# Expert stages of a two-layer trunk on one core: slot indices two units ahead, the transposed activations copied by ScalarE, folded stream factors, and one more weight buffer

## The chip, the core and the metric

The kernel runs on one core of a Trainium2 chip. The core has five instruction streams that run side by side and meet at semaphores: TensorE (PE in the profile, with its weight loads as PEld), VectorE (DVE), ScalarE (ACT), GpSimd (POOL) and SyncE (SP, which here issues nearly all DMAs). Matmul results land in PSUM, everything else lies in SBUF, and the weights are in HBM. The metric is the device time of one execution in microseconds (us); lower is better.

## The reference, cut to what matters

```python
def hier_moe(h, wg_r, bg_r, we_r, be_r, w_gate, w_up, w_down):
    # h: (T, 1024). Top-1 of 4 expert groups, then top-2 of the 8 experts in it.
    ...
    def expert(args):
        xb, e = args
        return (jax.nn.silu(xb @ w_gate[e]) * (xb @ w_up[e])) @ w_down[e]
    ys = lax.map(expert, (xs, blk_e)).reshape(slots, d)
    ys = ys * slot_w[:, None]
    return jax.ops.segment_sum(ys, slot_tok, num_segments=t + 1)[:t]

for layer in range(2):
    ...                                   # a mixer: even layer, odd layer
    x = x + mx[2] * yx
    if need_ctx:                          # layer 0: 256 latent and 256 context tokens
        y = hier_moe(tokens, *moe_params)
        x = x + mx[5] * y[:256]; xc = xc + mc[5] * y[256:]
    else:                                 # layer 1: 256 latent tokens
        x = x + mx[5] * hier_moe(hx2, *moe_params)
```

All is float32. Each layer has 32 experts, with three matrices of 2 MB each (gate and up 1024x512, down 512x1024), so a layer reads 201 MB of expert weights.

## The kernel before, in words

The program runs the even mixer, the expert stage of layer 0, the odd mixer, and the expert stage of layer 1, in this order; the text calls the two expert stages "layer 0" and "layer 1". The change touches the expert stages alone.

**Slots and units.** Each expert has 64 slots for the tokens sent to it. A **unit** is two experts, 128 slots; 16 units make a layer. In layer 0 a further unit of one expert (the fourth in order, the "extra" one) takes an expert that overflows its 64 slots. For a unit the kernel needs an **index**: `group` (L453) compares positions with slot numbers and gives, for four experts, one 0/1 tile `gt` per 128 tokens; `slot_sums` (L263) multiplies them with token numbers and routing weights on PE into the PSUM bank `mx`, DVE copies the sums out (L264) and makes the row list `ix` (L272) and the slot weights `ws` (L309), and POOL gathers the rows from HBM into one of two buffers `xg` (L275). `turned` transposes the rows on PE (L288) into `xT`.

**A unit on PE.** `hidden(j)` multiplies expert j's gate and up weights (L329, L330; 8 contraction steps c); ACT takes the silu (`sg`, L333), DVE the product `a` (L334). `turn` transposes `a` on PE into `mx` (L348), and a copy (L350) brings it to SBUF as `aT`. `down` multiplies with the down weights (L364) into the two banks `y`. Then ACT and DVE split `y` times the slot weight into two parts `yh`, `yl` (L378, L379), and `scatter` sends them back to the tokens: for each 128 tokens two pairs of matmuls with the 0/1 matrix `S` (L387, L388; `S` itself is made by `places`, L484 and L342), and the sum into `x_sb`. In layer 0 the result is first multiplied with a factor that depends on the stream, latent or context (`mx5`: L392), then added (L393, half of it on POOL). In layer 1 there is one stream, and the factor is folded into `y` (L373).

**The order on PE** is written out by hand (`manual_schedule`); the other engines' order is set by the build's scheduler, and each engine then takes its instructions strictly in that order. In step k of the main loop PE runs `hidden(0)` of unit k, with hooks after contraction step c (the index of unit k+1 at c=1, a scatter at c=3 and c=7), then `turn` and `down` of unit k-1, then `hidden(1)` of unit k with the transposes of the gathered rows of unit k+1. So a unit's down part stands in the middle of the next unit.

**Weights** come as 1 MB loads (L145) on SP's queue, six per expert, into a ring of buffers: 5 `w` and 8 `wx` in layer 0 (`NW`, `NX[0]`), 5 and 11 in layer 1. A load waits until PE is done with the buffer it overwrites. The order of the loads is that of use: gate and up of a unit's first expert, the four down loads of the unit before, gate and up of the second expert.

Of the kernel before, what the change touches and what calls it, by code (L numbers as in the profile page):

```python
# [34 lines left out]
NE = 32  # L35
# [2 lines left out]
GRP = 4  # L38
NW = 5
NX = (8, 11)  # L40
NZ = (0, 0)
EXTRA = 3
RP = 300
HP = 300
# [16 lines left out]
class Trunk:  # L61
# [247 lines left out]
            nc.vector.tensor_add(ws[r], wl[r, a:a + 1], wl[r, b:b + 1])  # L309
        return ws  # L310

    def unit(self, W, xT, slots, ws, posbc, NT, x_sb, mx5, last=False):

        nc = self.nc
        T = NT * 128
        u = {}

        def hidden(j, hooks=()):  # L320
            if "a" not in u:
# [22 lines left out]
        def turn():  # L344
            M = len(W()) * CAP
            pt = self.mps.tile([128, 512], F32, name="mx", bufs=1)
            for c in range(4):
                nc.tensor.transpose(pt[:, c * M:(c + 1) * M], u["a"][:M, c:512:4], self.ident[:M, :M])  # L348
            aT = u["aT"] = self.mp.tile([128, 4, M], F32, name="aT", bufs=2)
            nc.vector.tensor_copy(aT, pt[:, :4 * M].rearrange("p (c m) -> p c m", c=4))  # L350

        def down():
            ne = len(W())
            M = ne * CAP
            mz = mx5
            if last and len(mx5) == 2:
                mz = self.slot_mx5(u["S"], mx5)
            y = [self.mps.tile([128, 512], F32, name="y", bufs=2) for h in range(2)]
            for cc in range(2):
                for h in range(2):  # L360
                    for c in (2 * cc, 2 * cc + 1):
                        for j in range(ne):
                            r = slice(64 * j, 64 * j + 64)
                            nc.tensor.matmul(y[h][r], u["aT"][:, c, r], W()[j][2][cc][:, c % 2, 512 * h:512 * h + 512],  # L364
                                             start=(c == 0), stop=(c == 3))
            w = ws()[:M]
            ys = []
            for h in range(2):
                yh = self.mp.tile([128, 512], F32R, name=f"yh{h}", bufs=1)
                yl = self.mp.tile([128, 512], F32R, name=f"yl{h}", bufs=1)  # L370
                if len(mz) == 1:
                    yv = self.mp.tile([128, 512], F32, name="tm", bufs=2)
                    nc.vector.scalar_tensor_tensor(yv[:M], y[h][:M], w, mz[0][:M, 512 * h:512 * h + 512], op0=OP.mult,  # L373
                                                   op1=OP.mult)
                    nc.scalar.activation(yh[:M], yv[:M], AF.Copy)  # L375
                    (nc.vector if last else nc.gpsimd).tensor_tensor(yl[:M], yv[:M], f32(yh[:M]), op=OP.subtract)  # L376
                else:
                    nc.scalar.activation(yh[:M], y[h][:M], AF.Copy, scale=w)  # L378
                    nc.vector.scalar_tensor_tensor(yl[:M], y[h][:M], w, f32(yh[:M]), op0=OP.mult, op1=OP.subtract)  # L379
                ys.append((yh, yl))  # L380

            def scatter(t):
                for h, (yh, yl) in enumerate(ys):
                    i = 2 * t + h
                    s = u["S"][:M, t * 128:(t + 1) * 128]
                    p = self.mps.tile([128, 512], F32, name="gu" if last and i % 4 > 1 else "sc", bufs=2)
                    nc.tensor.matmul(p, s, yh[:M], start=True, stop=False)  # L387
                    nc.tensor.matmul(p, s, yl[:M], start=False, stop=True)  # L388
                    xv = x_sb[:, t, 512 * h:512 * h + 512]
                    if len(mz) == 2:  # L390
                        tm = self.mp.tile([128, 512], F32, name="tm", bufs=2)
# [12 lines left out]

    def slot_mx5(self, S, mx5):

        nc = self.nc
        v = self.mp.tile([128, 2], F32, name="sv")
        nc.vector.tensor_reduce(v, f32(S).rearrange("p (s t) -> p s t", s=2), axis=AX.X, op=OP.add)
        m = self.mp.tile([128, 8, 128], F32, name="xT", bufs=2).rearrange("p c n -> p (c n)")  # L410
# [29 lines left out]
    def moe(self, l, NT, pos, whl, counts, weights, first, posT, x_sb, mx5, early):  # L440
# [7 lines left out]
        def group(g):  # L448

            gts[g] = []  # L450
            for t in range(NT):
                x = self.mp.tile([128, GRP, CAP], F32R, name="gt", bufs=2 * NT)
                nc.vector.tensor_tensor(x, self.slotrow, pos[:, t, g * GRP:(g + 1) * GRP, None]  # L453
                                        .to_broadcast([128, GRP, CAP]), op=OP.is_equal)
                gts[g].append(x.rearrange("p a b -> p (a b)"))

        def inputs(p, ahead=True, banks=("xg",)):

            gt = [x[:, 128 * (p % 2):128 * (p % 2) + 128] for x in gts[p // 2]]
            have = {}  # L460
# [5 lines left out]
            def index():  # L466
                if ahead:
                    pw = self.slot_sums(NT, gt, whl, 128)
                    have["x"] = self.slot_rows(NT, pw[:, 64:66], 128)
                    weights_of(pw)  # L470
                else:
                    have["x"] = self.slot_rows(NT, self.slot_sums(NT, gt, whl[:, :, 64:66], 128), 128)

            xTs[p] = self.mp.tile([128, 8, 128], F32, name="xT", bufs=2)
            parts = [index] + self.turned(lambda: have["x"], 128, xTs[p], banks)
            if not ahead:
                parts.append(lambda: weights_of(self.slot_sums(NT, gt, whl, 128)))
            return parts

        def places(e):  # L480
            pb = self.mps.tile([128, 512], F32, name="mx", bufs=1)
# [4 lines left out]

        with tc.manual_schedule(engines={mybir.EngineType.PE}):
            with tc.high_priority(offset=RP):
                group(0)
                *parts, w0 = inputs(0, False, ("xg", "sc"))  # L490
                for f in parts:
                    f()
            weights()
            ov = self.overflow_list(NT, counts, self.mp)
# [10 lines left out]
            for p in range(NE // 2):  # L505
                units.append((p, self.unit(lambda k=len(units): self.W[k], lambda p=p: xTs[p], 0,
                                           lambda p=p: wss[p], lambda p=p: places(2 * p), NT, x_sb, mx5,
                                           p == NE // 2 - 1)))
# [11 lines left out]
            for k, (p, (hidden, place, turn, down)) in enumerate(units):  # L520
# [7 lines left out]
                            loaded.enter_context(tc.issue_after(i))  # L528
                elif k == 5:
                    loaded.close()  # L530
                if p is not None and p % 2 == 0 and p // 2 + 1 < NE // GRP:
                    group(p // 2 + 1)
                nxt = []
                if k + 1 < len(units):
                    q = units[k + 1][0]
                    nxt = extra[0] if q is None else inputs(q)
                if before:
                    hidden(0, {1: nxt[:1], 3: [lambda: some(scat), before[1]], 7: [lambda: some(scat)]})
                    before[2]()
                    some(scat, 9)  # L540
                    scat += before[3]()
                else:
                    hidden(0, {1: nxt[:1]})
                    w0()
                if p is None:
                    some(scat)
                    for f in nxt[1:]:
                        f()
                else:
                    lastp = [place] if k == len(units) - 1 else []  # L550
                    hidden(1, {2: nxt[1:2], 3: [lambda: some(scat)] + lastp, 6: nxt[2:], 7: [lambda: some(scat)]})
                before = hidden, place, turn, down
            some(scat, 9)
            turn()
            for f in down():
                f()
        early()
        self.epools = self.epools[NW:]
# [1639 lines left out]
```

## Time and profile before

| what | value |
|---|---|
| median of 3 runs | 1798.78 us (1796.64 to 1801.61) |
| the profiled execution | 1799.0 us, its span from first to last instruction 1797.2 us |
| PE, DVE, ACT, POOL busy | 1620.4, 855.2, 455.1, 363.6 us |
| mean granted clock of PE | 0.965 |
| moved by DMA | 521.2 MB, mean 290 GB/s |
| layer 0 on PE, first gate matmul to end of the last scatter | 428.9 to 966.7 us |
| layer 1 on PE, first down part to the last scatter | 1348.2 to 1787.7 us |

The span is counted from the first instruction; all times below are in us from there. The busy share of PE says little by itself, since an engine that waits for another inside each unit still shows nine tenths.

### The profile page before, as it was taken

What the parts mean: (1) busy time and instruction counts of PE and PEld (TensorE: products, weight loads), DVE (VectorE), ACT (ScalarE), POOL (GpSimd) and SP (SyncE); (2) the same over time, 40 slices, a digit from 0 to 9 for tenths busy, and PEclk for the clock granted to TensorE, in tenths of its full rate; (3) what the DMA queues carried; (4) which work ended last, traced back from release to release, by engine and by line L of the source; (5) the groups of instructions that cost most, each with busy time, mean ns of one, the idle gap of its engine ahead of it and who ended that gap; (6) DMA issues with size and microseconds to landing.
All of it is one profiled execution on the core that took longest, in us unless ns stands there. A gap on an engine that the chain in (4) does not pass through costs nothing. (4 is left out here: it accounts for less than half of the span.)

```text
span 1797.2 us, 21195 instructions
## 1 busy us (share of the span) xinstructions
PE 1620.4 (90%) x8160; PEld 878.7 (49%) x8160; DVE 855.2 (48%) x1685; ACT 455.1 (25%) x753; POOL 363.6 (20%) x340
## 2 busy tenths in 40 slices
PE   6999999896999989989897997998869999999996
PEld 4766778773333333333334864787623333333332
DVE  3236158786344444534446489666423333322232
ACT  2335245441111101111013563443311111111110
POOL 2102045311122221222214011322201111111100
PEclk9999999997999999999998998999879999999999
DMA  8755530347999999999973162501679999999995
GB/s 282 258 185 224 231 129 1 121 169 307 418 420 352 418 414 388 412 386 397 416 294 133 59 253 91 206 24 50 240 324 419 420 419 419 419 420 420 419 420 222
DMA packets 104586, 521.20 MB, mean 290 GB/s; under 512 B 19502, under 2 KB 29682, under 8 KB 49303
## 3 DMA queue, kind: packets, MB, share of 16 engines
q1 hardware_dynamic: 98924, 510.31, 71.4%
q0 software_dynamic: 4688, 6.30, 1.0%
q10 hardware_dynamic: 864, 3.15, 0.4%
q8 instruction: 66, 1.08, 0.3%
q14 instruction: 44, 0.36, 0.1%
HBM read 525.13 MB, written 5.33 MB: 295 GB/s over the span
## 5 line engine op out<-in xcount | busy, mean ns | idle before, releaser
L330 PE MATMUL gu<-wx,xT 128*64 128x512 f32 x704 | 332.7, 602 | 2.8 <-DMA wx<-moe_w_up_in 2.4
L329 PE MATMUL gu<-wx,xT 128*64 128x512 f32 x616 | 291.3, 601 | 0.0
L364 PE MATMUL y<-wx,aT 128*64 128x512 f32 x696 | 191.1, 613 | 39.2 <-DVE aT L350 33.4
L329 PE MATMUL gu<-w,xT 128*64 128x512 f32 x424 | 204.6, 609 | 0.0
L393 POOL TENSOR_TENSOR x_sb<-x_sb,tm 128x512 f32<-128x512 f32 x64 | 97.3, 1520 | 361.6 <-DVE tm L392 343.4
L330 PE MATMUL gu<-w,xT 128*64 128x512 f32 x336 | 161.5, 611 | 0.9 <-DMA w<-moe_w_up_in 0.9
L392 DVE TENSOR_TENSOR tm<-sc,mx 128x512 f32<-128x512 f32 x128 | 85.9, 689 | 143.7 <-PE sc L388 141.9
L329 PEld LDWEIGHTS gu<-wx,xT 128*64 128x64 f32 x616 | 74.9, 136 | 109.2 <-issue 105.9
L364 PEld LDWEIGHTS y<-wx,aT 128*64 128x64 f32 x696 | 59.8, 140 | 140.0 <-issue 88.0
L129 DVE TENSOR_TENSOR wl<-w,wh 128x1024 fp32r<-128x1024 f32 (+1 forms) x62 | 78.2, 1261 | 93.5 <-ACT wh L128 93.1
L364 PE MATMUL y<-w,aT 128*64 128x512 f32 x344 | 104.0, 619 | 15.9 <-DVE aT L350 15.2
L333 ACT ACTIVATE sg<-gu 64x512 f32<-64x512 f32 x65 | 38.4, 591 | 297.0 <-PE gu L330 297.0
L128 ACT ACTIVATE wh<-w 128x1024 fp32r<-128x1024 f32 (+1 forms) x72 | 75.0, 1048 | 129.6 <-PE acc L138 98.0
L330 PEld LDWEIGHTS gu<-wx,xT 128*64 128x64 f32 x704 | 85.3, 136 | 40.0 <-issue 31.7
L137 PE MATMUL acc<-wl,hT 128*128 128x512 f32 (+1 forms) x240 | 94.5, 394 | 0.0
L136 PE MATMUL acc<-wh,hT 128*128 128x512 f32 (+1 forms) x240 | 92.7, 400 | 0.0
L138 PE MATMUL acc<-wh,hT 128*128 128x512 f32 (+1 forms) x240 | 92.5, 392 | 0.0
L387 PE MATMUL sc<-yh,S 128*128 128x512 f32 (+1 forms) x194 | 87.2, 449 | 5.4 <-DVE tm L392 3.5
L329 PEld LDWEIGHTS gu<-w,xT 128*64 128x64 f32 x424 | 52.0, 138 | 71.7 <-issue 68.6
L376 POOL TENSOR_TENSOR yl<-tm,yh 128x512 fp32r<-128x512 f32 x30 | 38.1, 1270 | 210.6 <-ACT yh L375 210.6
L275 POOL DMA_INDIRECT xg<-h2d,ix x33 | 33.9, 1026 | 229.3 <-DVE ws L309 186.1
L298 DVE TENSOR_SCALAR xT<-xg,f1A,f1B 128x128 f32<-128x128 f32 x62 | 25.4, 410 | 114.8 <-PE xg L288 99.0
(642 smaller groups left out, 2930.5 us busy)
## 6 DMA issues: line engine op xcount, KB each, us to landing
wx<-moe_w_up_in SPq DMA_DIRECT2D x88, 1024.0 KB
wx<-moe_w_down_in SPq DMA_DIRECT2D x87, 1024.0 KB
wx<-moe_w_gate_in SPq DMA_DIRECT2D x77, 1024.0 KB
w<-moe_w_gate_in SPq DMA_DIRECT2D x53, 1024.0 KB
w<-ada_w_in SPq DMA_DIRECT2D x48, 1024.0 KB
w<-moe_w_down_in SPq DMA_DIRECT2D x43, 1024.0 KB
w<-moe_w_up_in SPq DMA_DIRECT2D x42, 1024.0 KB
w<-even_w_in_in SPq DMA_DIRECT2D x14, 1024.0 KB
```

What stands on the lines that cost most here:

```text
L128: nc.scalar.activation(hv, src, AF.Copy)
L129: self.lo_eng[0].tensor_tensor(lv, src, f32(hv), op=OP.subtract)
L136: mm(ps, a[0], b[0], start=start, stop=False)
L137: mm(ps, a[0], b[1], start=False, stop=False)
L138: mm(ps, a[1], b[0], start=False, stop=stop)
L329: nc.tensor.matmul(g, xs[:, c, :], G[c // 4][:, c % 4, :], start=(c == 0), stop=(c == 7))
L330: nc.tensor.matmul(v, xs[:, c, :], U[c // 4][:, c % 4, :], start=(c == 0), stop=(c == 7))
L333: nc.scalar.activation(sg[64 * j:64 * j + 64], g, AF.Silu)
L364: nc.tensor.matmul(y[h][r], u["aT"][:, c, r], W()[j][2][cc][:, c % 2, 512 * h:512 * h + 512], start=(c == 0), stop=(c == 3))
L387: nc.tensor.matmul(p, s, yh[:M], start=True, stop=False)
L392: nc.vector.tensor_mul(tm, p, mx5[t // 2][:, 512 * h:512 * h + 512])
L393: (nc.gpsimd if h else nc.vector).tensor_add(xv, xv, tm)
```

## The change

- `index_of` takes the place of the first part of `inputs`. The index of unit k+2 now stands right behind the `turn` of unit k-1 and ahead of its `down`, instead of the index of unit k+1 after c=1 of `hidden(0)`. The tiles `gt` have `NT` buffers instead of `2 * NT`; `group` is called by the index that first needs it.
- The copy of `aT` out of PSUM is an ACT instruction instead of a DVE one.
- `slot_mx5`, which folds the two stream factors into one per slot, is used for the last two units of layer 0 instead of the last one, and writes into the unit's `xg` buffer.
- After the main loop the last `turn` comes first, then one remaining scatter, `down`, the other remaining scatters.
- `NZ = (1, 0)`: layer 0 gets a fourteenth weight buffer, `wz`. Its first load is issued after the buffers of the stage before are released.

```diff
-NZ = (0, 0)
+NZ = (1, 0)
...
-            nc.vector.tensor_copy(aT, pt[:, :4 * M].rearrange("p (c m) -> p c m", c=4))
+            nc.scalar.activation(aT, pt[:, :4 * M].rearrange("p (c m) -> p c m", c=4), AF.Copy)
...
-            if last and len(mx5) == 2:
-                mz = self.slot_mx5(u["S"], mx5)
+            if end >= 0 and len(mx5) == 2:
+                mz = self.slot_mx5(u["S"], mx5, row())
...
-                x = self.mp.tile([128, GRP, CAP], F32R, name="gt", bufs=2 * NT)
+                x = self.mp.tile([128, GRP, CAP], F32R, name="gt", bufs=NT)
...
+        def index_of(p, ahead=True):
+            if p // 2 not in gts:
+                group(p // 2)
             gt = [x[:, 128 * (p % 2):128 * (p % 2) + 128] for x in gts[p // 2]]
...
+            if not ahead:
+                rows[p] = self.slot_rows(NT, self.slot_sums(NT, gt, whl[:, :, 64:66], 128), 128)
+                return lambda: weights_of(self.slot_sums(NT, gt, whl, 128))
+            pw = self.slot_sums(NT, gt, whl, 128)
+            rows[p] = self.slot_rows(NT, pw[:, 64:66], 128)
+            weights_of(pw)
...
-                if p is not None and p % 2 == 0 and p // 2 + 1 < NE // GRP:
-                    group(p // 2 + 1)
...
                 if before:
-                    hidden(0, {1: nxt[:1], 3: [lambda: some(scat), before[1]], 7: [lambda: some(scat)]})
+                    hidden(0, {3: [lambda: some(scat), before[1]], 7: [lambda: some(scat)]})
                     before[2]()
+                    index(k + 2)
                     some(scat, 9)
                     scat += before[3]()
                 else:
-                    hidden(0, {1: nxt[:1]})
+                    hidden(0, {1: [lambda: index(1)]})
                     w0()
+                    index(2)
...
+            turn()
+            some(scat)
+            end = down()
             some(scat, 9)
-            turn()
-            for f in down():
+            for f in end:
                 f()
```

How this moves instructions shows at three places. First PE in the middle of layer 0, before: the index stands inside `hidden(0)`,

```order
L329 MATMUL gu<-wx,xT 64x512
L330 MATMUL gu<-wx,xT 64x512
L263 MATMUL mx<-r_whl,gt 128x66 x4
L329 MATMUL gu<-wx,xT 64x512
L330 MATMUL gu<-wx,xT 64x512
```

and at the turn of the same unit the transposes (L348) are followed at once by the down part:

```order
L387 MATMUL sc<-yh_5286,S 128x512
L388 MATMUL sc<-yl_5287,S 128x512
L387 MATMUL sc<-yh_5290,S 128x512
L388 MATMUL sc<-yl_5291,S 128x512
L348 MATMUL mx<-c_ident,a 128x128 x4
L364 MATMUL y<-wx,aT 64x512 x8
```

The same turn of the changed kernel, whose lines are numbered two higher here:

```order
L389 MATMUL sc<-yh_5304,S 128x512
L390 MATMUL sc<-yl_5305,S 128x512
L389 MATMUL sc<-yh_5308,S 128x512
L390 MATMUL sc<-yl_5309,S 128x512
L350 MATMUL mx<-c_ident,a 128x128 x4
L263 MATMUL mx<-r_whl,gt 128x66 x4
L366 MATMUL y<-w,aT 64x512
L366 MATMUL y<-wx,aT 64x512
```

The four index matmuls have moved between the transposes and the down part; they write the one bank `mx`, which the copy of `aT` reads.

Second, DVE around the same turn, before: the copy of `aT` stands behind the scatter's products and sums and the product `a`.

```order
L334 TENSOR_TENSOR a<-sg,gu 64x512
L392 TENSOR_TENSOR tm<-sc,mx_1_2841 128x512
L393 TENSOR_TENSOR x_sb<-x_sb,tm 128x512
L350 COPY aT<-mx 128x512
L379 SCALAR_TENSOR_TENSOR yl_5451<-y,ws,yh_5450 128x512
L379 SCALAR_TENSOR_TENSOR yl_5455<-y,ws,yh_5454 128x512
```

In the changed kernel the copy is gone from there, and the index's own DVE work (the copy of the sums, `ix`, `ws`) has come in:

```order
L336 TENSOR_TENSOR a<-sg,gu 64x512
L394 TENSOR_TENSOR tm<-sc,mx_1_2841 128x512
L395 TENSOR_TENSOR x_sb<-x_sb,tm 128x512
L454 TENSOR_TENSOR gt<-c_srow,r_pos 128x256 x3
L264 COPY wl<-mx 128x66
L454 TENSOR_TENSOR gt<-c_srow,r_pos 128x256
L272 SCALAR_TENSOR_TENSOR ix<-wl 128x1
L309 TENSOR_TENSOR ws<-wl 64x1 x2
L381 SCALAR_TENSOR_TENSOR yl_5305<-y,ws,yh_5304 128x512
L381 SCALAR_TENSOR_TENSOR yl_5309<-y,ws,yh_5308 128x512
```

Every second turn has the `gt` rows; three of the four stand ahead of the copy of this index's sums, so they are the compares of the next group, made one unit before an index reads them.

Third, PE at the end of layer 0, before: all scatters that are left come ahead of the last transposes (L348).

```order
L387 MATMUL sc<-yh_6542,S 128x512
L388 MATMUL sc<-yl_6543,S 128x512
L387 MATMUL sc<-yh_6546,S 128x512
L388 MATMUL sc<-yl_6547,S 128x512
L348 MATMUL mx<-c_ident,a 128x128 x4
L364 MATMUL y<-wx,aT 64x512
L364 MATMUL y<-w,aT 64x512
```

Of the changed kernel, from the last scatter inside `hidden(1)` on:

```order
L389 MATMUL sc<-yh_6555,S 128x512
L390 MATMUL sc<-yl_6556,S 128x512
L350 MATMUL mx<-c_ident,a 128x128 x4
L389 MATMUL sc<-yh_6549,S 128x512
L390 MATMUL sc<-yl_6550,S 128x512
L389 MATMUL sc<-yh_6555,S 128x512
L390 MATMUL sc<-yl_6556,S 128x512
L366 MATMUL y<-wx,aT 64x512
L366 MATMUL y<-wz,aT 64x512
```

One remaining scatter now lies between the transposes and the down part, and the other one behind the down part.

## Rows read from the trace of the kernel before

**Rows 1.** The page's first two lines: the span, and each engine's busy time, share of the span and instructions.

```profile
span 1797.2 us, 21195 instructions
PE 1620.4 (90%) x8160; PEld 878.7 (49%) x8160; DVE 855.2 (48%) x1685; ACT 455.1 (25%) x753; POOL 363.6 (20%) x340
```

**Rows 2.** Busy time by stretch: the middle of layer 0 and of layer 1. After the stretch (us from the span's start) and its length come busy us of PE, PEld, DVE, ACT and POOL with their instructions, the granted PE clock (1.00 is full speed), the busy share of the DMA engines, and GB/s moved.

```profile
436.00:930.00 494.00, 456.59 (x2003) 174.52 (x2001) 217.75 (x360) 59.50 (x95) 110.29 (x89) 0.99 0.98 401
1328.00:1764.00 436.00, 414.16 (x1789) 149.45 (x1785) 135.69 (x278) 64.26 (x121) 54.99 (x57) 1.00 1.01 419
```

**Rows 3.** The list of waits, by engine and line that waited and what it waited for: us in total, times, the longest. The first row is layer 0 (437 to 960 us), the second layer 1 (1310 to 1798 us).

```profile
PE y L364 <- DVE aT L350: 36.1, 16, 2.5
PE y L364 <- DVE aT L350: 12.5, 16, 0.8
```

**Rows 4.** The same list for SP's queue, which issues the weight loads (L145): first in layer 0, then in layer 1.

```profile
SPq L145 <- PE gu L330: 258.1, 62, 7.8
SPq L145 <- DMA wx<-moe_w_down_in: 76.2, 34, 3.6
```

**Rows 5.** The timeline of one turn in layer 0: start, duration, engine, line, what is written and read, and in brackets how long the engine had been idle and what ended it.

```profile
699.94 0.59 ACT L333 ACTIVATE sg<-gu 64x512 f32<-64x512 f32 x1 [9.97 <-PE gu L330]
700.56 0.69 DVE L392 TENSOR_TENSOR tm<-sc,mx 128x512 f32<-128x512 f32 x1 [1.75 <-PE sc L388]
700.84 0.63 PE L348 MATMUL mx<-c_ident,a 128*128 128x128 f32 x4
702.61 0.68 DVE L393 TENSOR_TENSOR x_sb<-x_sb,tm 128x512 f32<-128x512 f32 x1
703.21 0.68 DVE L350 COPY aT<-mx 128x512 f32<-128x512 f32 x1
703.95 3.65 PE L364 MATMUL y<-wx,aT 128*64 128x512 f32 x16 [2.48 <-DVE aT L350]
```

**Rows 6.** The timeline of one turn in layer 1.

```profile
1537.89 0.75 PE L348 MATMUL mx<-c_ident,a 128*128 128x128 f32 x4
1539.42 2.80 PE L364 MATMUL y<-w,aT 128*64 128x512 f32 x12 [0.78 <-DVE aT L350]
```

**Rows 7.** Prices. The first two rows are groups of one form in layer 0 (times | busy us, mean ns of one | idle before): ACT's copy of a 128x512 tile out of PSUM, and DVE's copy of `aT`. Then PE's timeline around one index inside `hidden(0)`.

```profile
L290 ACT ACTIVATE xT<-xg 128x512 f32<-128x512 f32 x30 | 17.9, 597 | 103.4 <-PE xg L288 103.4
L350 DVE COPY aT<-mx 128x512 f32<-128x512 f32 x16 | 10.9, 683 | 4.2 <-PE mx L348 4.2
723.05 0.59 PE L329 MATMUL gu<-wx,xT 128*64 128x512 f32 x1
723.58 0.64 PE L263 MATMUL mx<-r_whl,gt 128*128 128x66 f32 x4
724.15 0.64 PE L329 MATMUL gu<-wx,xT 128*64 128x512 f32 x1
```

**Rows 8.** DVE's timeline: the copies of `aT` of the two units before the one of Rows 5.

```profile
638.82 0.68 DVE L350 COPY aT<-mx 128x512 f32<-128x512 f32 x1
670.17 0.68 DVE L350 COPY aT<-mx 128x512 f32<-128x512 f32 x1
```

**Rows 9.** Stretches as in Rows 2: the first and the last of four short ones in layer 0 in which the clock fell, the last turn of layer 0, and all turns of layer 1.

```profile
574.00:578.50 4.50, 3.35 (x12) 1.08 (x14) 1.10 (x2) 0.00 (x0) 1.62 (x1) 0.75 1.01 421
830.00:834.50 4.50, 3.45 (x12) 1.20 (x14) 0.99 (x2) 0.00 (x0) 1.52 (x1) 0.75 1.00 415
946.00:954.00 8.00, 6.23 (x18) 2.54 (x18) 4.80 (x8) 0.00 (x0) 4.67 (x3) 0.65 0.01 2
1335.00:1788.00 453.00, 427.67 (x1840) 154.85 (x1836) 141.96 (x285) 66.04 (x123) 56.32 (x59) 1.00 0.98 406
```

**Rows 10.** The timeline of the end of layer 0.

```profile
941.16 0.59 PE L329 MATMUL gu<-wx,xT 128*64 128x512 f32 x1
942.32 0.60 ACT L333 ACTIVATE sg<-gu 64x512 f32<-64x512 f32 x1
942.33 1.28 DVE L412 SCALAR_TENSOR_TENSOR xT<-mx,sv,xT 128x1024 f32<-128x1024 f32 x1 [1.22 <-ACT xT L411]
944.24 0.68 DVE L334 TENSOR_TENSOR a<-sg,gu 64x512 f32<-64x512 f32 x1
949.03 1.06 PE L348 MATMUL mx<-c_ident,a 128*128 128x128 f32 x4
950.87 1.12 PE L364 MATMUL y<-wx,aT 128*64 128x512 f32 x1 [0.78 <-DVE aT L350]
958.41 0.75 DVE L373 SCALAR_TENSOR_TENSOR tm<-y,ws,xT 128x512 f32<-128x512 f32 x1 [6.40 <-PE y L364]
966.05 0.69 DVE L399 TENSOR_TENSOR x_sb<-x_sb,gu 128x512 f32<-128x512 f32 x1
```

**Rows 11.** The start of layer 0: SP's last load that finds a free buffer and the first that reuses one, then PE and DVE around the second index.

```profile
402.56 0.46 SPq L145 DMA_DIRECT2D wx<-moe_w_down_in  x1
435.20 0.81 SPq L145 DMA_DIRECT2D w<-moe_w_down_in  x2
438.54 0.63 PE L263 MATMUL mx<-r_whl,gt 128*128 128x66 f32 x4
440.03 0.42 DVE L453 TENSOR_TENSOR gt<-c_srow,r_pos 128x256 fp32r<-128x256 f32 x1
```

**Rows 12.** A stretch as in Rows 2: the end of the weight loads of layer 0.

```profile
920.00:940.00 20.00, 17.52 (x81) 6.71 (x79) 8.23 (x12) 1.97 (x3) 3.15 (x3) 1.00 0.58 227
```

More of the change, by code (lines that the diff above doesn't have):

```diff
@@ L310, in slot_weights, with unit @@
         return ws
-    def unit(self, W, xT, slots, ws, posbc, NT, x_sb, mx5, last=False):
+    def unit(self, W, xT, slots, ws, posbc, NT, x_sb, mx5, end=-1, row=None):
         nc = self.nc
@@ L318, in unit @@
         u = {}
+        last = end == 1
         def hidden(j, hooks=()):
@@ L403, in unit, with slot_mx5 @@
         return hidden, places, turn, down
-    def slot_mx5(self, S, mx5):
+    def slot_mx5(self, S, mx5, m):
         nc = self.nc
-        v = self.mp.tile([128, 2], F32, name="sv")
+        v = self.mp.tile([128, 2], F32, name="sv", bufs=2)
         nc.vector.tensor_reduce(v, f32(S).rearrange("p (s t) -> p s t", s=2), axis=AX.X, op=OP.add)
-        m = self.mp.tile([128, 8, 128], F32, name="xT", bufs=2).rearrange("p c n -> p (c n)")
         nc.scalar.activation(m, mx5[0], AF.Copy, scale=v[:, 0:1])
@@ L455, in group @@
                 gts[g].append(x.rearrange("p a b -> p (a b)"))
-        def inputs(p, ahead=True, banks=("xg",)):
+        rows = {}
+        def index_of(p, ahead=True):
+            if p // 2 not in gts:
+                group(p // 2)
             gt = [x[:, 128 * (p % 2):128 * (p % 2) + 128] for x in gts[p // 2]]
-            have = {}
             def weights_of(pw):
@@ L464, in weights_of, with inputs @@
                 wss[p] = self.slot_weights(pw, [(i, 32 + i), (i + 1, 33 + i)])
[L466 to L472, printed above, removed]
+            if not ahead:
[4 more added lines that the diff above has]
+            weights_of(pw)
+        def inputs(p, banks=("xg",)):
             xTs[p] = self.mp.tile([128, 8, 128], F32, name="xT", bufs=2)
[L475 to L478, printed above, removed]
+            return self.turned(lambda: rows[p], 128, xTs[p], banks)
         def places(e):
@@ L488, in moe @@
             with tc.high_priority(offset=RP):
-                group(0)
-                *parts, w0 = inputs(0, False, ("xg", "sc"))
-                for f in parts:
+                w0 = index_of(0, False)
+                for f in inputs(0, ("xg", "sc")):
                     f()
@@ L507, in moe @@
                                            lambda p=p: wss[p], lambda p=p: places(2 * p), NT, x_sb, mx5,
-                                           p == NE // 2 - 1)))
+                                           p - NE // 2 + 2, lambda p=p: rows[p])))
                 if first and len(units) == EXTRA:
@@ L535, in moe, with index @@
                     q = units[k + 1][0]
-                    nxt = extra[0] if q is None else inputs(q)
+                    nxt = extra[0][1:] if q is None else inputs(q)
+                def index(k):
+                    if k < len(units):
+                        q = units[k][0]
+                        if q is None:
+                            extra[0][0]()
+                        else:
+                            index_of(q)
                 if before:
-                    hidden(0, {1: nxt[:1], 3: [lambda: some(scat), before[1]], 7: [lambda: some(scat)]})
+                    hidden(0, {3: [lambda: some(scat), before[1]], 7: [lambda: some(scat)]})
                     before[2]()
+                    index(k + 2)
                     some(scat, 9)
@@ L542, in moe @@
                 else:
-                    hidden(0, {1: nxt[:1]})
+                    hidden(0, {1: [lambda: index(1)]})
                     w0()
+                    index(2)
                 if p is None:
                     some(scat)
-                    for f in nxt[1:]:
+                    for f in nxt:
                         f()
@@ L550, in moe @@
                     lastp = [place] if k == len(units) - 1 else []
-                    hidden(1, {2: nxt[1:2], 3: [lambda: some(scat)] + lastp, 6: nxt[2:], 7: [lambda: some(scat)]})
+                    hidden(1, {2: nxt[:1], 3: [lambda: some(scat)] + lastp, 6: nxt[1:], 7: [lambda: some(scat)]})
                 before = hidden, place, turn, down
+            turn()
+            some(scat)
+            end = down()
             some(scat, 9)
-            turn()
-            for f in down():
+            for f in end:
                 f()
```

## The prediction

> **What bounds the kernel now.** The page's first two lines give PE 90 % of the span and no other engine half of it [rows 1], so I asked stage by stage whether PE or the weights end last. The stretches differ [rows 2]: the middle of layer 0 moves 401 GB/s with PE busy 456.59 of 494.00 us; that of layer 1 moves 419 GB/s at a DMA share of 1.01. The waits say which side is ahead. In layer 0 the load queue waits for PE to hand back buffers, 62 times, 258.1 us [rows 4], while PE waits 36.1 us in 16 waits, all of them for DVE's copy of `aT` [rows 3]. In layer 1 the queue's largest wait is for earlier transfers [rows 4], and PE's wait for the copy is 12.5 us [rows 3]. So layer 0 is bound by PE and its turns; layer 1 by its transfers, which start when that stage starts. Its turns can be shortened without moving its end, except behind the last load.
>
> The timeline of a turn shows why layer 0 pays three times as much [rows 5]. The transposes end at 700.84 + 0.63 = 701.47. DVE, strictly in order, still has a scatter's product (700.56), the product `a` and a scatter's sum (702.61) around them, and starts the copy at 703.21. PE idles 2.48 us. In layer 1 the same wait is 0.78 us [rows 6].
>
> **The turn, 14 units.** On ACT nothing stands between `sg`, which ends at 699.94 + 0.59 = 700.53, and the copy; ACT had idled 9.97 us before [rows 5] and is busy 59.50 of 494 us [rows 2]. Its copy of a 128x512 tile out of PSUM takes 597 ns; DVE's copy 683 [rows 7]. A gap of 0.78 with a copy of 0.68 leaves 0.10 for the two hand-overs [rows 6, 7], so ACT's gap is 0.70. I take it (with a copy as slow as DVE's it would be 0.78, 1.1 us over 14 turns). Of 16 waits, 36.1 us, the first and the last are 0.78, the other 14 thus 2.47 to 2.48: 14 x (2.48 - 0.70) = **24.9 us**.
>
> **The index.** Its four matmuls lengthen the pitch of `hidden(0)` from 0.53 or so (723.58 - 723.05, one matmul pair) to a resumption at 724.15, 0.57 us after the index began [rows 7]. That goes from `hidden(0)` and comes behind the turn. It needs the one `mx` bank, so it runs after the copy and not inside the gap. Net nothing. Its reads (`gt`) are made a unit earlier; its results are wanted a unit later, so the gather loses no time. The second `slot_mx5` (a 1.28 us row like [rows 10] on DVE, and ACT work) lies in DVE's free half [rows 2]; with that cover gone it would cost 1.3 to 3 us, once.
>
> **The clock.** Four times in layer 0 the granted clock falls after a turn: 4.5 us at 0.75, a mean of the two levels 1.2 and 2.4 GHz [rows 9], where the first and the last of the four stand. The copies of `aT` are 31.35 us apart without a dip (638.82 to 670.17) and 33.04 with one (670.17 to 703.21) [rows 8, 5]: 1.69 us each. Layer 1, with the same turns at 0.78 idle, holds 1.00 throughout [rows 9]. At 0.70 I expect none: 4 x 1.69 = **6.8 us**; bounds 0 and 6.8, the nearer row being layer 1's.
>
> **The end of layer 0.** Before, `hidden(1)` ends at 941.75, the remaining scatters run, the turn comes at 949.03, and `down` at 950.87: 9.1 us; the stretch 946 to 954 then has a clock of 0.65 [rows 10, 9]. After: `sg` 942.4, `a`, which DVE can begin behind the 1.28 us `slot_mx5` at about 943.4 or with a scatter's product in between, ends near 944.05, transposes to 944.75, copy to 945.4, one scatter meanwhile, `down` at about 945.75. That is 5.1 us earlier. With PE then busy, I count the half-clock part of `down` back, about 4 us of it, 2.0. Behind `down` DVE has the last scatter's products ahead of `yl` (before, that chain began at 958.41 [rows 10]): two of about 0.65, so minus 1.3. Together **5.8 us**, bounds 3.1 (no clock, and as much again lost on DVE) and 7.1.
>
> **The start.** The index of unit 2 now stands behind the first unit's slot weights. It needs `mx` free and the fourth `gt`, at 440.03 + 0.42 = 440.45 [rows 11], so `hidden(1)` begins near 440.65, not 439.11 (where the index of 438.54 had run [rows 11] and gone): 1.5 later, less 0.6 for the index itself: **minus 0.9 us**.
>
> **Can the weights follow?** From 436 to 930 layer 0 moves 401 x 0.494 = 198.1 MB [rows 2], and 227 x 0.020 = 4.5 MB are in the last stretch [rows 12]. At layer 1's 419 to 420 GB/s the 198.1 MB take 472 us: the end falls from 930 to 908, and the last load lands there. PE wants that load for its last `down`, at 950.87 - 36 = 915. A unit has 31.35 - 1.78 = 29.6 us on PE and 12.9 MB (201 MB by 16, and some 0.3 MB of gathered rows, an estimate), 30.7 us of DMA at 420. So the queue's lead, some 12 loads in the ring, shrinks about 0.4 load a unit, to some 8 of 14 at the end. The margin is 6 to 9 us. `wz` adds one load of lead; its first load falls in the pause of the queue between 402.56 and 435.20 [rows 11] and delays nothing. Without `wz` the margin would be some 2.4 us less, still positive.
>
> The Trainium skill ("DMA: Bandwidth & Descriptors", "Where 436 GB/s comes from") gives the ceiling on the way into SBUF as 435 GB/s. This trace shows 419 at a full share [rows 2]; by the page's figure the 198.1 MB would take an estimated 455 us and the margin would be larger.
>
> Layer 1 is worth 0.1 us at its tail, one gap of 0.78 made 0.70 [rows 6]; the rest of its 16 gaps is hidden by the transfers.
>
> **Sum.** 24.9 + 6.8 + 5.8 - 0.9 = 36.6 us. The profiled execution took 1799.0, the median is 1798.78, so no correction: **1762.5 us**. A difference of 0.3 % (5.4 us) is about what a measurement of this kernel can tell from none.
>
> **Rivals.** *The clock dips stay, or others take their place* (0.12). There is still an idle in every turn, and at the end one copy's worth. Against it stands layer 1's 1.00 [rows 9]. The price is the 6.8 us: 1769.3. The Trainium skill ("TensorE: Matmul & The Clock Gate", "A second HAM failure mode: psum-queue depth-cycling") says that short idles between groups of matmuls can make the clock swing between its levels. Layer 1's row speaks against it for idles of 0.78 us, and layer 0's rows show the fall after idles of 2.48.
>
> *The loads become the bound in layer 0* (0.12). If the queue cannot use the time that PE returns (it still waits for buffers in places, and each wait costs transfer time), the DMA keeps its loss of 494 x (420 - 401)/420 = 22 us, of which it now has room to lose only 6 to 9. If it keeps 20, the last loads land near 927, 12 us after PE wants them, and the gain is some 27: 1772. For it: a share of 0.98 at 401 GB/s [rows 2], which reads as if little were free. Against it: the queue's waits for PE, 258.1 us [rows 4], are the very thing that shortens.
>
> *PE waits for the index instead* (0.07, slower). PE takes instructions in order, so an index whose `gt` or sums come late holds `down`. If DVE makes the compares behind the scatter's sum, the fourth would end at 703.21 + 1.57 + 0.63 = 705.4, counting the three before it at about 0.52 each and the last in shared time, where `down` began at 703.95 before [rows 5]. It decides only if the compares end after about 704, that is over 2.5 us behind the transposes. It would take the turns from 2.48 to 3.3 us (16 x 0.8 = 12.7 us lost), a dip a turn at 1.69 for the 12 that have none now (20.3 us), less the end's 5.8: about 1826. Against it: the listing has three of the four compares one unit ahead of their reader, and DVE is idle over half of the time [rows 2].
>
> *No measurable change* (0.05): the gain of the turns is given back in layer 1 or in the mixer between, which would need that stage to wait for something other than layer 0's end. I see nothing that does; its loads find free buffers early, as layer 0's do [rows 11].
>
> **How the numbers follow.** The forecast has 0.64, own range 1757 (end at its best, an extra 4 us from faster steps) to 1767.5 (dips half kept, the end at 3.1, copy at 0.68). With both rivals at 1769 and 1772 the range 1756 to 1772 holds about 0.8. Faster by over 0.3 %: 0.64 + 0.12 + 0.12 = 0.88; same 0.05; slower 0.07.
>
> **What would show it.** In the changed profile PE's wait for `aT` in layer 0 should be 16 x 0.7 = 11 us and name ACT; copies of `aT` should be 29.6 us apart, with no dip; the middle of layer 0 should show 418 or more GB/s and the load queue should wait for transfers, not for PE; `down` should begin about 4 us after the last `hidden(1)` ends; the length of layer 1 should be the same. The forecast is wrong if PE in layer 0 waits for a load, for `gt` or for `ix`, or if the clock in `hidden` falls below 1.00.

## The result and the profile after

The changed kernel takes 1758.84 us (median; 1757.78 to 1761.0), the kernel before in the same session 1800.19: a ratio of 0.9775 (95 % interval 0.9756 to 0.9793), 41.4 us faster. The forecast was 1762.5 us, in a range of 1756 to 1772. Profiled executions: 1799.0 us before and 1757.8 after, spans 1797.2 and 1755.9.

The page of the changed kernel, first lines, against [rows 1]:

```profile
span 1755.9 us, 21166 instructions
PE 1604.4 (91%) x8160; PEld 877.9 (50%) x8160; DVE 833.6 (47%) x1650; ACT 475.3 (27%) x787; POOL 361.3 (21%) x338
```

The middle of layer 0 and of layer 1, columns as in [rows 2]:

```profile
436.00:892.00 456.00, 443.30 (x1983) 172.85 (x1979) 208.94 (x346) 68.13 (x110) 110.47 (x88) 1.00 1.01 418
1310.00:1723.00 413.00, 392.37 (x1692) 144.28 (x1689) 118.88 (x246) 68.17 (x126) 52.35 (x54) 1.00 1.01 419
```

Layer 0 now moves 418 GB/s in place of 401, as fast as layer 1, and its clock is 1.00 throughout this stretch. PE's waits for `aT` in layer 0 (first for the index behind the turn, then for the down part), and those of the load queue, answer to [rows 3, 4]:

```profile
PE mx L263 <- ACT aT L352: 9.4, 14, 0.7
PE y L366 <- ACT aT L352: 1.4, 2, 0.7
```

```profile
SPq L145 <- PE gu L332: 180.6, 50, 7.1
SPq L145 <- DMA wx<-moe_w_down_in: 30.4, 15, 2.1
```

PE's 36.1 us have become 10.8. One turn in the timeline, against [rows 5], with the copy of the unit before it:

```profile
657.34 0.60 ACT L352 ACTIVATE aT<-mx 128x512 f32<-128x512 f32 x1 [0.97 <-PE mx L350]
...
686.11 0.63 PE L350 MATMUL mx<-c_ident,a 128*128 128x128 f32 x4
686.57 0.69 DVE L336 TENSOR_TENSOR a<-sg,gu 64x512 f32<-64x512 f32 x1
686.78 0.60 ACT L352 ACTIVATE aT<-mx 128x512 f32<-128x512 f32 x1 [0.97 <-PE mx L350]
687.29 0.69 DVE L394 TENSOR_TENSOR tm<-sc,mx 128x512 f32<-128x512 f32 x1
687.43 0.63 PE L263 MATMUL mx<-r_whl,gt 128*128 128x66 f32 x4 [0.69 <-ACT aT L352]
687.89 0.68 DVE L395 TENSOR_TENSOR x_sb<-x_sb,tm 128x512 f32<-128x512 f32 x1
687.99 0.64 PE L366 MATMUL y<-w,aT 128*64 128x512 f32 x1
```

The scatter's product and sum still stand on DVE at 687.29 and 687.89; nobody waits for them any more. The copies are 29.44 us apart (657.34 to 686.78) in place of 31.35 or 33.04. The end of layer 0, against [rows 10]:

```profile
908.70 0.59 ACT L335 ACTIVATE sg<-gu 64x512 f32<-64x512 f32 x1 [0.69 <-PE gu L332]
910.01 0.68 DVE L336 TENSOR_TENSOR a<-sg,gu 64x512 f32<-64x512 f32 x1
910.75 0.75 PE L350 MATMUL mx<-c_ident,a 128*128 128x128 f32 x4 [1.04 <-DVE a L336]
912.35 0.64 PE L366 MATMUL y<-wx,aT 128*64 128x512 f32 x1
926.06 0.69 DVE L401 TENSOR_TENSOR x_sb<-x_sb,gu 128x512 f32<-128x512 f32 x1
```

**Where the 41.3 us of span went**, from the two timelines:

| stretch | before | after | difference |
|---|---|---|---|
| to the first gate matmul of layer 0 | 428.86 | 429.63 | +0.8 |
| to the first copy of `aT` | 27.69 | 27.54 | -0.15 |
| to the last but one copy in layer 0 | 468.82 | 435.11 | -33.7 |
| to the last sum into `x_sb` of layer 0 | 42.16 | 35.26 | -6.9 |
| to the first copy in layer 1 | 379.93 | 380.92 | +1.0 |
| to the last copy in layer 1 | 428.34 | 428.68 | +0.3 |
| to the end | 21.39 | 18.80 | -2.6 |

The first row is not the change's: in the fourteen profiles here (two kernels, twelve experiments) layer 0 starts anywhere from 425.2 to 434.9 us. So the time of one execution carries some us that no edit made, and below the stretches of the traces are compared first, the medians of four executions second.

### The profile page after: what moved, and what is told of

Same layout as the page of the kernel before. It is cut to its first block, busy times and chain, and to the rows that moved or that the text cites. A ratio compares the mean times of both kernels' runs of the same rounds, so it can differ in the third digit from the quotient of the medians.

```text
span 1755.9 us, 21166 instructions
## 1 busy us (share of the span) xinstructions
PE 1604.4 (91%) x8160; PEld 877.9 (50%) x8160; DVE 833.6 (47%) x1650; ACT 475.3 (27%) x787; POOL 361.3 (21%) x338
## 5 line engine op out<-in xcount | busy, mean ns | idle before, releaser
L332 PE MATMUL gu<-wx,xT 128*64 128x512 f32 x672 | 314.5, 603 | 7.2 <-DMA wx<-moe_w_up_in 6.8
L331 PE MATMUL gu<-wx,xT 128*64 128x512 f32 x576 | 269.9, 602 | 0.0
L394 DVE TENSOR_TENSOR tm<-sc,mx 128x512 f32<-128x512 f32 x120 | 80.1, 688 | 159.4 <-PE sc L390 158.5
L395 POOL TENSOR_TENSOR x_sb<-x_sb,tm 128x512 f32<-128x512 f32 x60 | 92.5, 1542 | 292.3 <-DVE tm L394 289.6
L331 PEld LDWEIGHTS gu<-wx,xT 128*64 128x64 f32 x576 | 71.6, 136 | 104.2 <-issue 98.5
L332 PEld LDWEIGHTS gu<-wx,xT 128*64 128x64 f32 x672 | 83.5, 137 | 47.1 <-issue 33.2
L331 PEld LDWEIGHTS gu<-w,xT 128*64 128x64 f32 x464 | 57.5, 137 | 85.1 <-issue 79.8
L366 PE MATMUL y<-w,aT 128*64 128x512 f32 x280 | 79.9, 596 | 1.4 <-ACT aT L352 1.4
L390 PE MATMUL sc<-yl,S 128*128 128x512 f32 (+1 forms) x194 | 77.3, 398 | 1.8 <-DVE yl L378 1.0
L336 DVE TENSOR_TENSOR a<-sg,gu 64x512 f32<-64x512 f32 x65 | 44.6, 686 | 70.3 <-ACT sg L335 68.8
```

The costliest lines, as they stand in the source:

```text
L331: nc.tensor.matmul(g, xs[:, c, :], G[c // 4][:, c % 4, :], start=(c == 0), stop=(c == 7))
L332: nc.tensor.matmul(v, xs[:, c, :], U[c // 4][:, c % 4, :], start=(c == 0), stop=(c == 7))
```

## Experiments

**The copy alone, the index alone, the copy taken back.** The kernel before with only the ACT copy (`b_act`):

```diff
-            nc.vector.tensor_copy(aT, pt[:, :4 * M].rearrange("p (c m) -> p c m", c=4))
+            nc.scalar.activation(aT, pt[:, :4 * M].rearrange("p (c m) -> p c m", c=4), AF.Copy)
```

> The kernel before with one edit: the copy of aT is an ACT instruction. Theory (the idle of each turn is the whole story, and the clock falls because of it): 14 turns x 1.79 us (2.48 to 0.69) = 25.1, four clock dips of 1.69 = 6.8, so about 32 us faster than before, 1768 us, with no dip in layer 0 and copies of aT 29.5 to 29.6 us apart. Rival A (the dips come from something that is still there, such as the index inside hidden(0)): 25 us faster, 1775, dips still there. Rival B (without the fourteenth buffer the loads can't follow): 1775 to 1780, PE waiting for loads in the last units of layer 0.

Measured: 1768.44 us, ratio 0.9798 (0.9772 to 0.9825). The middle of layer 0 is at 1.00, and PE's waits for `aT` are 11.0 us:

```profile
460.00:895.00 435.00, 423.40 (x1878) 162.93 (x1878) 200.45 (x326) 63.32 (x103) 107.09 (x86) 1.00 1.01 419
```

The copies are 29.56 us apart, no dip, and with thirteen buffers next to no wait for loads. A dip is a short stretch in which the granted clock is at half. Rivals A and B fall: this one line is worth 33 of the 41 us in the medians. By the trace, 31.7 of it lie between the first and the last but one copy in layer 0 (437.14 us in place of 468.82), idle and dips together; 2.7 lie in the tail (below).

The changed kernel with only its index kept (`b_index`: DVE copy, `NZ = (0, 0)`, `slot_mx5` for the last unit alone, old end):

> The changed kernel with everything taken back but the index: it stands two units ahead behind the turn; the copy of aT is on DVE, thirteen buffers, the end of layer 0 as before. Theory: behind the turn the index costs 0.56 us and inside hidden(0) it cost 0.67, so 14 x 0.11 = 1.5 us gained, 0.6 lost at the start; within 2 us of the kernel before, about 1799, dips and the 2.48 us waits unchanged. Rival (the index holds the down part, as PE takes instructions in order): PE waits for gt or for the copy in each turn, 1810 or more.

Measured: 1811.72 us against 1801.42, ratio 1.005 (1.0025 to 1.0074). Slower, but not as the rival had it: PE waits for `aT` as long as before (14 times, 32.0 us, and twice, 5.0). The clock is what changed. Four pieces of 1.5 us after one turn, whose idle ended at about 741.0, and the same four after the next turn, without a dip:

```profile
740.26:741.76 1.50, 0.76 (x4) 0.77 (x4) 0.99 (x3) 0.00 (x0) 1.20 (x1) 0.56 1.02 421
741.76:743.26 1.50, 1.50 (x6) 0.69 (x7) 1.49 (x8) 0.00 (x0) 0.00 (x0) 0.50 1.00 415
743.26:744.76 1.50, 1.50 (x6) 0.39 (x4) 0.06 (x1) 0.00 (x0) 1.02 (x1) 0.50 0.99 410
744.76:746.26 1.50, 1.50 (x6) 0.32 (x4) 0.00 (x0) 0.00 (x0) 0.00 (x0) 0.50 0.90 352
...
774.54:776.04 1.50, 0.76 (x6) 0.72 (x8) 0.78 (x3) 0.00 (x0) 1.20 (x1) 1.00 1.01 421
776.04:777.54 1.50, 1.50 (x8) 0.43 (x6) 0.51 (x4) 0.00 (x0) 0.90 (x1) 1.00 1.00 415
777.54:779.04 1.50, 1.50 (x10) 0.57 (x8) 0.00 (x0) 0.00 (x0) 0.12 (x1) 1.00 1.04 431
779.04:780.54 1.50, 1.50 (x10) 0.43 (x7) 0.00 (x0) 0.00 (x0) 0.00 (x0) 1.00 0.89 320
```

At 0.50 (1.2 GHz) the `down` part does 6 matmuls in a piece where it does 8 to 10 at 1.00 (2.4 GHz). Between copies of `aT` it is 31.24 us without a dip, 32.93 or 34.28 with one: dips of 1.69 and now of 3.04, in eight of the first fifteen intervals, 20 us in all, where the kernel before has four of 1.69. First to last copy in layer 0 is 505.3 us against 493.6. So behind turns that idle 2.48 us the move of the index costs 11.7 us in layer 0; the same move behind short turns gains 2.0 (below). That the clock makes the difference is shown; why the index behind a long idle brings more and longer dips, and which turns get one, is not.

The changed kernel with DVE's copy back (`a_dve`, the first diff reversed):

> The changed kernel with one edit taken back: the copy of aT is on DVE again. Theory: the turns wait 2.48 us again in 14 units (25.1 us) and four to six dips come back (6.8 to 10 us); about 1791 to 1795. Rival (the index move and the new end carry a good part of the gain): 1780 or less.

Measured: 1804.22 us, ratio to the kernel before 1.0023 (1.0004 to 1.0042). The theory's size was 10 us too small, for the same reason: dips in eight of the first fifteen intervals, with 32.93 and 34.28 again between copies.

**Is it the idle, or DVE?** `a_act4` makes ACT's copy four times in a row (`for _ in range(4):` ahead of it), `a_act2` twice.

> The changed kernel in which ACT makes the copy of aT four times in a row, so that each turn idles 2.49 us with DVE out of it. Theory (the clock falls because of the length of the idle in a turn): 14 x 1.8 = 25.2, both ends 3.6 and four to six dips of 1.69 = 6.8 to 10, so 1794 to 1798, with dips in layer 0 and now in layer 1 too. Rival (the dips belong to DVE's order around the turn and not to PE's idle): 1787.6 and no dip.

> The changed kernel in which ACT makes the copy of aT twice, so that a turn idles 1.29 us: between the 0.69 that showed no dip and the 2.49 that showed one in half the turns of layer 0 or more. If 1.29 us brings no dip: 14 x 0.60 = 8.4, both ends 1.2, 1768 to 1769, copies of aT 30.0 us apart. If it brings dips in a third of the turns or more: 1775 and up.

Measured: 1831.74 us (ratio 1.0157) and 1770.68 (0.984). Layer 0 and layer 1 of the first, then layer 0 of the second:

```profile
457.00:920.00 463.00, 423.65 (x1828) 164.05 (x1825) 184.86 (x319) 89.04 (x147) 104.57 (x83) 0.97 0.97 393
1390.00:1770.00 380.00, 347.33 (x1480) 123.27 (x1480) 104.41 (x217) 83.24 (x150) 48.60 (x50) 0.95 1.01 418
```

```profile
457.00:892.00 435.00, 414.01 (x1848) 161.73 (x1845) 196.01 (x322) 72.92 (x119) 106.36 (x84) 1.00 1.01 417
```

With ACT alone making the idle, now 2.57 us, layer 0 has the same kinds of dip as with DVE (31.32 between copies without, 33.02 and 34.33 with). So the length of the idle matters and not who makes it, though not the length alone, since with the same idle some turns dip and others do not. The size was missed by 34 us or more. Layer 1 gave 20 of it (448.97 us from its first copy to its last in place of 428.68), with a dip in nearly every unit: 30.59 us a unit in place of 27.02 in its first six, until PE and no longer the loads sets that layer's pace. Layer 0 gave some 10: 45.5 us longer from first copy to last (499.87 in place of 454.37), where 32 to 35 were forecast. At 1.29 us of idle (14 waits, 18.0 us) there is no dip in layer 0: 30.07 between copies, that is 29.44 + 0.63, as forecast for that case; the median is 2 us above it.

**The loads.** `a_nz0` has `NZ = (0, 0)`, `a_nx5` also `NX = (5, 11)`. `a_xg` lets the index run inside the idle, in a bank of its own:

```diff
-        pw = self.mps.tile([128, 512], F32, name="mx", bufs=1)[:M, 0:R]
+        pw = self.mps.tile([128, 512], F32, name="xg", bufs=1)[:M, 0:R]
```

> The changed kernel with thirteen weight buffers in layer 0 in place of fourteen. Theory (margin of 6 to 9 us, one load is 2.5 us): no change that can be measured, 1758 to 1760. Rival (the fourteenth buffer is what lets the loads follow): 1761 to 1765 and PE waits for loads at the end of layer 0.

> The changed kernel with ten weight buffers in layer 0 in place of fourteen: four loads or 10 us of lead less. Theory (margin of 6 to 9 us): the last units wait for loads, 1 to 4 us lost, 1760 to 1763. Rival A (the lead is ample): 1759. Rival B (a ring below the twelve loads of a unit stalls in every unit): 1780 or more.

> The changed kernel with the sums of the index in the bank xg in place of mx, so that the index runs inside the idle of the turn, while ACT copies aT. PE then has 0.56 us less in each of 14 units (7.8 us). Theory (the loads of layer 0 end only some 6 to 9 us before PE wants them): about 5 to 7 us are gained before PE waits for loads; 1752 to 1754, and the load queue waits for transfers almost throughout. Rival A (the loads bind already): no gain, 1758 to 1759. Rival B (layer 1's start or the clock takes it): the gain shows at the end of layer 0 and not at the end of the kernel.

Measured: 1759.40, 1759.89 and 1754.35 us. First to last copy in layer 0: 454.37 us in the changed kernel, 454.36 without the fourteenth buffer, 460.91 with ten, 451.14 with the index in the idle. With ten buffers PE's weight loads wait for transfers (first row), and with the faster PE as well (second):

```profile
810.52 0.13 PEld L332 LDWEIGHTS gu<-wx,xT 128*64 128x64 f32 x1 [1.36 <-DMA wx<-moe_w_up_in]
```

```profile
895.52 0.13 PEld L332 LDWEIGHTS gu<-wx,xT 128*64 128x64 f32 x1 [0.78 <-DMA wx<-moe_w_up_in]
```

The two give the margin from both sides. Four loads less are 4 x 2.5 = 10 us of lead, and 6.5 were lost: 3.5 us of margin. `a_xg` runs at 28.87 between copies, 0.57 x 14 = 8.0 us less work for PE; its last three intervals before the end stretch to 30.59, 30.34 and 20.24, and 3.2 us remain: 3.2 of margin. Both theories had the direction right. The time of `a_nx5` shows only 1 us of its loss: the profiled execution (1758.71 us) began layer 0 at 425.2, the earliest of all, and of the other three there is no trace. `a_xg` is the fastest kernel here, 4.5 us below the changed one in the medians (ratio 0.9751, 0.9729 to 0.9774, which overlaps), 3.2 us in layer 0 by the trace.

**The end of layer 0.** `a_end` takes back the order at the end, `a_one` the second `slot_mx5`; `b_two` is the kernel before with the ACT copy and `slot_mx5` for two units.

```diff
-            turn()
-            some(scat)
-            end = down()
             some(scat, 9)
-            for f in end:
+            turn()
+            for f in down():
```

```diff
-            if end >= 0 and len(mx5) == 2:
+            if end == 1 and len(mx5) == 2:
```

> The changed kernel with the old order at the end of each layer: all scatters that are left, then the last turn. Theory (5.1 us earlier down part, the clock's part, less 1.3 on DVE): 5 to 6 us slower, 1764 to 1765, with the last two copies of aT in layer 0 24.8 us apart in place of 19.3. Rival (what is won before the down part is lost behind it on DVE): within 2 us, 1759 to 1761.

> The changed kernel in which slot_mx5 is used for the last unit of layer 0 alone, as before; the last turn still comes first. Theory A (the prediction's: the turn put first earns the gain at the end of layer 0, and slot_mx5 is worth nothing): 1758 to 1760. Theory B (formed from the run with the old end: from the last copy but one of aT in layer 0 to the first in layer 1 it took 416.1 us like the changed kernel, and 423 with neither edit, so the folded factors of the last but one unit earn it): about 6 us slower, 1764 to 1766, that stretch 421 to 423 us.

> The kernel before with two edits alone: the copy of aT by ACT, and slot_mx5 for the last two units of layer 0. The index, the thirteen buffers and the order at the end are as before. Theory B: the stretch around the end of layer 0 falls from 423 to 416 us, 1761 to 1763, within 3 us of the changed kernel. Theory A: no more than the ACT copy alone, 1768.

Measured: 1762.31, 1764.10 and 1760.07 us; part of the differences is the start and single dips (`a_one`'s layer 0 has two). None of the forecasts held in full. The last two copies of `a_end` are 21.96 us apart, where 24.8 were forecast. The stretch from the last but one copy to layer 1 takes 417.8 us in `a_one` and 418.6 in `b_two`, between the 416 and the 421 to 423 by which theories A and B were to be told apart. By the trace, from the end of the last `hidden(1)` to the last sum into `x_sb` of layer 0:

| | old end | turn first |
|---|---|---|
| `slot_mx5` for the last unit | 26.4 (`b_act`; 25.8 before) | 22.2 (`a_one`) |
| for the last two | 20.8 (`a_end`), 20.7 (`b_two`) | 18.95 (changed kernel) |

Each number is one execution. The 22.2 of `a_one` hold 3.4 us at half clock behind its `down` part (0.50 from 933.4 to 936.8), so some of its distance to 18.95 is the clock. From that last sum to the first copy of layer 1 it takes 379.0 (`a_end`) to 381.9 us (`a_act4`) in the fourteen profiles: differences of 2 us at the end of layer 0 cannot be told in the times of whole executions.

Why, shows in `b_act`'s timeline and in `b_two`'s at the scatters between the last `hidden(1)` and the last turn:

```profile
915.88 0.50 PE L387 MATMUL sc<-yh,S 128*128 128x512 f32 x1 [1.38 <-DVE tm L392]
916.57 0.69 DVE L392 TENSOR_TENSOR tm<-sc,mx 128x512 f32<-128x512 f32 x1
917.18 0.68 DVE L393 TENSOR_TENSOR x_sb<-x_sb,tm 128x512 f32<-128x512 f32 x1
917.34 1.65 POOL L393 TENSOR_TENSOR x_sb<-x_sb,tm 128x512 f32<-128x512 f32 x1 [5.77 <-DVE tm L392]
...
920.79 1.05 PE L348 MATMUL mx<-c_ident,a 128*128 128x128 f32 x4
922.53 1.11 PE L364 MATMUL y<-wx,aT 128*64 128x512 f32 x1 [0.69 <-ACT aT L350]
```

```profile
912.27 0.50 PE L388 MATMUL sc<-yh,S 128*128 128x512 f32 x1 [0.31 <-DVE x_sb L400]
912.96 1.28 DVE L400 TENSOR_TENSOR x_sb<-x_sb,sc 128x512 f32<-128x512 f32 x2
913.70 0.50 PE L388 MATMUL sc<-yh,S 128*128 128x512 f32 x1 [0.70 <-DVE x_sb L400]
```

The scatters that are left are those of the last but one unit. Unfolded, each half costs DVE a product and half the time a sum, and a POOL sum of 1.65 us; PE waits for them, and the clock is at half when the turn comes (1.05 for four transposes, 1.11 for a matmul). Folded, it is one DVE sum per half (L400 in `b_two`), and the clock stays. Either edit earns most of the gain alone; together they earn less than their sum (4.2 and 5.7 apart, 7.4 together).

**The tail.** In the changed kernel the output leaves at once behind DVE's last sum; in the kernel before 2.67 us later (1787.76 + 0.69 to 1791.12). Before, after, and `a_tail`, which is the changed kernel with one tiny DVE memset more in each `turn`:

> The changed kernel with one more DVE instruction in every turn (a memset of one column that nothing reads), so that DVE's program is as long as with the copy of aT on it. Theory (where DVE's program has to be fetched at its last jump is set by its length): the 2.4 to 2.7 us between DVE's last sum and the issue of the output come back, some 21 us from the last copy of aT to the end. Rival (the executed copies on DVE make it): 18.7 us as in the changed kernel.

```profile
1787.76 0.69 DVE L399 TENSOR_TENSOR x_sb<-x_sb,gu 128x512 f32<-128x512 f32 x1 [0.25 <-PE gu L388]
1791.12 0.82 SPq L2167 DMA_DIRECT2D out_dram<-x_sb  x2
```

```profile
1748.98 0.69 DVE L401 TENSOR_TENSOR x_sb<-x_sb,gu 128x512 f32<-128x512 f32 x1 [0.24 <-PE gu L390]
1749.76 1.23 SPq L2179 DMA_DIRECT2D out_dram<-x_sb  x2
```

```profile
1748.84 0.69 DVE L402 TENSOR_TENSOR x_sb<-x_sb,gu 128x512 f32<-128x512 f32 x1 [0.24 <-PE gu L391]
1752.18 0.82 SPq L2180 DMA_DIRECT2D out_dram<-x_sb  x2
```

The wait of the queue that issues the output, and one of the two instruction queues in the last 17 us (its packets, MB, and share of the time), both of `a_tail`:

```profile
SPq L2180 <- DVEq L660: 16.7, 1, 16.7
```

```profile
q14 instruction: 5, 0.04, 0.8%
```

With the memsets the 2.65 us are back, though the copy is still ACT's (1759.86 us in one execution). The output waits for DVE's sequencer (16.7 us here, 14.2 in the changed kernel). The instruction queue has 5 packets here and in the kernel before, 4 in the changed one. The other profiles agree: the four with 1683 to 1685 DVE instructions (`before`, `b_index`, `a_dve`, `a_tail`) have 2.4 to 2.7 us between DVE's last sum and the output, the ten with 1650 to 1652 have 0.08 or 0.09. So the length of DVE's program sets it; that DVE then fetches its code behind the jump over the skipped overflow branch is what the extra packet suggests, not what these rows prove.

## Why the prediction was right, point by point

- **The turns.** Forecast 0.70 us of idle and 24.9 us; measured 0.69 and, over the fifteen intervals, 33.7 less 6.8 for the dips, so 26.9. The copy alone (`b_act`) gives 31.7 there, the sum of the two terms as forecast. The 2.0 more are the index (437.14 us in `b_act`, 435.12 in the changed kernel), which was put at nothing: behind the turn it takes 687.99 - 687.43 = 0.56 us, inside `hidden(0)` it had cost 0.67. The prediction read 0.53 as the pitch of the matmul pairs there; they are 0.43 apart, the next was due at 723.48 and came at 724.15 [rows 7]. The 29.56 of `b_act` against 29.44 show the 0.12 a unit.
- **The clock.** 6.8 us as forecast, no dip left between the first and the last copy in layer 0. The rival that they stay falls. The Trainium skill ("TensorE: Matmul & The Clock Gate", "A second HAM failure mode: psum-queue depth-cycling") says that short idles between groups of matmuls make the clock swing; the runs agree for 2.5 us, and show it only now and then after 0.7 (in the last section) and not at all in layer 0 after 1.3.
- **The end of layer 0.** 5.8 forecast, 6.9 measured. The three terms were near: `down` begins 3.8 us after the last `hidden(1)` in place of 9.1, so 5.4 earlier (5.1 forecast); it takes 7.1 us (912.35 to 919.4) in place of 9.2, so 2.1 for the clock (2.0); behind it 0.65 is lost (1.3). The cause was half wrong: the step that lets the second `slot_mx5` lie in DVE's free half and cost nothing looked only at its cost. What it takes away, the products and POOL's sums in the last scatters, earns 5.7 us with the old end and 3.2 with the new one; the turn put first earns 4.2 or 1.8.
- **The start.** Minus 0.9 forecast; plus 0.15 measured from the first gate matmul. The step was right and the rest is luck. In the changed kernel PE waits for the bank behind the first unit's slot weights and then runs the moved index:

```profile
438.26 0.63 PE L263 MATMUL mx<-r_whl,gt 128*128 128x66 f32 x4
439.88 0.63 PE L263 MATMUL mx<-r_whl,gt 128*128 128x66 f32 x4 [0.99 <-DVE wl L264]
```

From there to the first copy of `aT` it takes 18.9 us (438.26 to 457.17), before 18.0 (438.54 [rows 11] to 456.55): the 0.9 that was forecast. It is 18.0 again in `b_act` and `b_two`, which have the old index, and 18.9 in the others with the moved one in the bank `mx`. What gave 1.05 back is the clock. Of the first 4 us from the first gate matmul it was at half throughout before (first row), and for 1.8 us in the changed kernel (second):

```profile
428.86:432.86 4.00, 4.00 (x11) 1.16 (x11) 1.06 (x6) 0.60 (x1) 0.00 (x0) 0.50 0.00 0
429.63:433.63 4.00, 4.00 (x17) 1.58 (x18) 0.52 (x4) 1.88 (x2) 0.00 (x0) 0.77 0.00 0
```

In `b_index`, `a_end` and `a_one`, which have the moved index too, the half clock lasts 3.5 to 3.9 us; so this is the execution and not the edit, as far as the runs show.

- **The weights.** That they can follow, with a small margin, was right; 6 to 9 us was too much, the two runs say 3.2 to 3.5. PE came to its last `down` at 912.35, 2.7 us ahead of the 915 that was taken; and 0.4 load a unit over some fifteen units takes 6 of the 12 loads of lead, not the 4 that the prediction took off. What makes up the rest is open. The load queue was to wait for transfers and not for PE: it still waits 180.6 us for PE, nearly all of it ahead of 812 us, from where loads leave 2.5 us apart. The rival of a binding load was therefore nearer than its 0.12 looked.
- **The rival of the late index** (PE waits for it) did not occur, but the same edit without the ACT copy is slower by another way, the clock.
- **The tail** was missed: 0.1 forecast, 2.6 measured. The four terms that were too small or left out (index 2.0, end 1.1, start 1.05, tail 2.5) add to 6.7; the later mixer, layer 1 and the start of layer 0 gave 2.1 back, and 36.6 became 41.2 of the 41.3. Neither the 1.05 nor the 2.1 is shown to come from an edit; without both, the second execution would have been 42.3 us shorter than the first.

## What to carry to other kernels

When an engine idles in a loop, price the clock beside the idle itself, and shorten the idle before work is moved behind it: the same index move gained 2 us behind 0.7 us of idle and lost 11.7 behind 2.5. When a step is called free because an idle engine does it, ask also whose work it removes. When one side of a pipeline is sped up, work out how late the other side may be; here 3 us were left, and more PE speed is lost to loads.

## What the runs showed that was not expected

- With the index behind it, an idle of 2.48 us brought dips that cost 3.04 us beside those that cost 1.69; without the index only the latter, and in fewer units. The short idles are not quite safe either. In three kernels built on the changed one (`a_end`, `a_one`, `a_tail`) the third interval between copies, beside the extra unit, is 24.7 to 24.9 us with a clock of 0.93, where it is 23.2 without a dip. `a_one` has one more dip in an ordinary unit, 31.14 us in place of 29.44, behind an idle of 0.69.
- Layer 1 of the changed kernel has one dip, behind a third kind of idle: PE waits 2.10 us for a load until 1604.73, and the clock is at 0.55 from 1605.5 to 1609.3. The interval between copies is 33.01 us there and the next 28.99, so the loads, which bind that layer, hide it.
- Thirty-odd instructions more or less in DVE's program moved the output by 2.3 to 2.6 us.
- The weight ring of layer 0 can give up its fourteenth buffer without loss (454.36 against 454.37 us), and four of them for 6.5 us.
